# The order in which TensorE reads its operands: interleaved halves, and weights 32 bytes apart

## Chip, cores and metric

The kernel runs on one core of one Trainium2 chip. The metric is the device time of one launch in microseconds (us); lower is better. Before the change the median of three runs is 2053.01 us (2051.42 to 2057.7).

## What is computed

The reference is one layer of an encoder for one sequence of 256 tokens and 2048 features, in float32. Cut to what matters:

```python
mod = silu(c) @ ada_w + ada_b                    # shift/scale/gate, six rows of 2048
h = rms_norm(x) * (1 + scale_m) + shift_m
proj = h @ w_in                                  # q,k,v,o,i,f | qkv,z,beta,a | merge gates
y_a = (sigmoid(a_o) * norm(mlstm both ways(q, k, v, i, f))) @ w_branch_a
qkv = silu(centred depthwise conv(b_qkv))        # along the tokens, 5 taps
y_b = (norm(gated delta rule both ways(qkv, beta, a)) * silu(b_z)) @ w_branch_b
x = x + gate_m * ((g_a * y_a + g_b * y_b) @ w_out)
hf = rms_norm(x) * (1 + scale_f) + shift_f
gt, up = split(hf @ w_gate_up)
x = x + gate_f * ((silu(gt) * up) @ w_down)      # 5632 features in between
out = rms_norm(x)
```

Nearly all the arithmetic is in the products with the large weight matrices.

## The kernel before

Every large product but the first stage's is made in fp32r, a type of float32 that TensorE reads in one pass, and made precise by splitting both factors into a high and a low part: high times high, high times low, low times high, three matmuls into the same PSUM accumulator. The activations are split once (`hh`, `hl` for the block's input, `hah`/`hal`, `obh`/`obl`, `mgh`/`mgl`, `hfh`/`hfl`, `ffh`/`ffl` later); the weights are split as they arrive: a DMA on the SP queue brings 1 MB into a tile `raw` (three buffers), ScalarE copies half of it to `wh` (fp32r), VectorE subtracts to get `wl`, and TensorE reads both (three buffers each).

There are two kinds of products.

*Products by feature* (`fjob`, lines 173 to 193) give a block of 128 features by 256 tokens. The weights are the stationary operand, 128 columns, and the activation `hh[:, kk]` or `hl[:, kk]`, 256 tokens, is the moving one; 16 blocks of the contraction, three matmuls each. They serve q, k and v of the delta rule (`b_job`, 36 blocks; `gdn_conv`, line 315, copies the accumulator into a padded tile and convolves along the tokens) and q and k of the mLSTM (`a_qk`, 13 blocks; `keep_f`, line 355, copies the accumulator out and stores it).

*Products by token* (`tjob`, lines 195 to 257) give 256 tokens, two halves of 128, by 512 features. Here the activation is the stationary operand (128 tokens) and the weights, 512 columns, are the moving one. A piece of weights is `[128, 4, 512]`; `halves` (line 203) makes `wh` and `wl` for two blocks of the contraction, and 12 matmuls read them (lines 230 to 232). The last product of the output projection and of the down projection is ordered by token half (`by_token`, lines 242 to 257), one of them with 256 columns at a time. Products by token are the gates z and o, v, the two merge gates, both branch projections, the output projection, and gate, up and down of the feed-forward part.

The stages in order: a first stage to about 138 us which makes the input `hh`, `hl` and the first 16 blocks by feature in plain fp32 (line 557); the delta rule with four groups of four heads, whose small steps are interleaved by hand-written counts (`fill`, `pump`, `stream`, `drive`) with products from a list, so that TensorE always has some; the mLSTM in the same way; the branch projections; the output projection; the feed-forward part from about 1307 us; and the last norm. Rows of the modulation (`ada`) are reduced on VectorE in between.

The host side prepares the weights once, before the launch: `_blocks` for weights by feature, `_groups` (line 1449) for weights by token, and a transposition for gate and up (`gu`).

Of the kernel before, what the change touches and what calls it, by code (L numbers as in the profile page):

```python
# [9 lines left out]
F32 = mybir.dt.float32  # L10
F32R = mybir.dt.float32r
AF = mybir.ActivationFunctionType
ALU = mybir.AluOpType
PSUM = bass.MemoryType.PSUM

P = 128
T = 256
D = 2048
KB = D // P
# [33 lines left out]
def hybrid_block(ctx: ExitStack, tc: tile.TileContext, xr, nfr, crow, pk_d, cst_d, ada2, ada4, win0, winb, wint, wba, wbb, wo, wgu, wd, out, dbg=None):  # L53
    nc = tc.nc
    V, S, G, PE = nc.vector, nc.scalar, nc.gpsimd, nc.tensor

    def pool(stack, name, bufs=1, **kw):
        return stack.enter_context(tc.tile_pool(name=name, bufs=bufs, **kw))

    cp = pool(ctx, "cp")  # L60
    st = pool(ctx, "st")
# [6 lines left out]
    def big(p, dt, name):  # L68
        return p.tile([P, KB, T], dt, tag="b16", name=name)

    def order(ins, yes=True):

        return tc.keep_in_program_order(ins) if yes else ins
# [33 lines left out]
    def add():  # L107

        part, b, raw = asked.pop(0)
        c = part * KB + b  # L110
        order(V.scalar_tensor_tensor(raw, raw, 1.0, row_c[:, :D], ALU.mult, ALU.mult, accum_out=mod[:, c : c + 1]), room[0][3] > 1)  # L111
        if b == KB - 1:
            c = slice(part * KB, part * KB + KB)
            V.tensor_tensor(mod[:, c], mod[:, c], pk[:, PK_ADAB + c.start : PK_ADAB + c.stop], ALU.add)
# [21 lines left out]
    def raw_tile(shape, name):  # L136

        since[0] += 1
        if since[0] > 2 and asked and room[0][0] is st:
            add()  # L140
        return st.tile(shape, F32, tag="raw", bufs=3, name=name)
# [31 lines left out]
    def fjob(name, src, done):  # L173

        ps = acc_ps.tile([P, 512], F32, tag="acc", name=f"acc_{name}")
        o = ps[:, :T]
        raw = raw_tile([P, KB, P], f"raw_{name}")
        nc.sync.dma_start(raw, src)
        for k0 in range(0, KB, 8):
            wh = st.tile([P, 8, P], F32R, tag="wh", bufs=3, name=f"wh_{name}_{k0}")  # L180
            wl = st.tile([P, 8, P], F32R, tag="wl", bufs=3, name=f"wl_{name}_{k0}")
            S.activation(wh, raw[:, k0 : k0 + 8], AF.Copy)
            settle()
            V.tensor_tensor(wl, raw[:, k0 : k0 + 8], wh.bitcast(F32), ALU.subtract)
            for k in range(8):
                kk = k0 + k
                PE.matmul(o, wh[:, k], hh[:, kk], start=kk == 0, stop=False)  # L187
                PE.matmul(o, wh[:, k], hl[:, kk], start=False, stop=False)  # L188
                PE.matmul(o, wl[:, k], hh[:, kk], start=False, stop=kk == KB - 1)  # L189
            if k0:  # L190
                pump()
                done(o)
            yield True

    def tjob(name, chunks, xh, xl, done, early=0, by_token=None, steps=1, parts=((0, slice(0, 512)), (1, slice(0, 512)))):

        raws = {}

        def halves(u, k0):
            if u not in raws:
                raws[u] = raw_tile([P, 4, 512], f"raw_{name}_{u}")
                nc.sync.dma_start(raws[u], chunks[u])
            wh = st.tile([P, 2, 512], F32R, tag="wh", bufs=3, name=f"wh_{name}_{u}_{k0}")
            wl = st.tile([P, 2, 512], F32R, tag="wl", bufs=3, name=f"wl_{name}_{u}_{k0}")
            order(S.activation(wh, raws[u][:, k0 : k0 + 2], AF.Copy), early)  # L209
            settle()  # L210
            order(V.tensor_tensor(wl, raws[u][:, k0 : k0 + 2], wh.bitcast(F32), ALU.subtract), early)  # L211
            return wh, wl

        todo = [(u, k0) for u in range(len(chunks)) for k0 in (0, 2)]
        made = []
        for i, q in enumerate(todo[:early]):
            made.append(halves(*q))
            if steps > 1 or i == early - 1:
                yield True
        ps = [acc_ps.tile([P, 512], F32, tag="acc", name=f"acc_{name}_{t}") for t in range(2)]  # L220
        last = 4 * len(chunks) - 1
        if by_token:
            todo = todo[:-2]
        for n, (u, k0) in enumerate(todo):
            wh, wl = made.pop(0) if made else halves(u, k0)
            for k in range(2):
                kk = 4 * u + k0 + k
                for t in range(2):
                    c = slice(t * P, (t + 1) * P)
                    order(PE.matmul(ps[t], xh[:, kk, c], wh[:, k], start=kk == 0, stop=False), early and steps > 1)  # L230
                    PE.matmul(ps[t], xl[:, kk, c], wh[:, k], start=False, stop=False)  # L231
                    PE.matmul(ps[t], xh[:, kk, c], wl[:, k], start=False, stop=kk == last)  # L232
            if k0:
                pump()
                if u == len(chunks) - 1:
                    done(ps)
            yield True
            if early and steps > 1:
                if n + early < len(todo):
                    made.append(halves(*todo[n + early]))  # L240
                yield True
        if by_token:
            w = [halves(len(chunks) - 1, k0) for k0 in (0, 2)]
            by_token()
            for i, (t, part) in enumerate(parts):
                if i > 1:
                    ps.append(acc_ps.tile([P, 512], F32, tag="acc", name=f"acc_{name}_{i}"))
                c = slice(t * P, (t + 1) * P)
                o = ps[i][:, : part.stop - part.start]
                for k in range(4):  # L250
                    kk = last - 3 + k
                    wh, wl = (a[:, k % 2, part] for a in w[k // 2])
                    PE.matmul(o, xh[:, kk, c], wh, start=i == 2 and not k, stop=False)
                    PE.matmul(o, xl[:, kk, c], wh, start=False, stop=False)
                    PE.matmul(o, xh[:, kk, c], wl, start=False, stop=kk == last)
                done(t, ps[i], part)
                yield True
# [34 lines left out]
    hh = big(bigA, F32R, "hh")  # L292
    hl = big(bigA, F32R, "hl")
# [9 lines left out]
    for i in range(NP_):  # L303
        pd = fr.tile([P, T + 4], F32, name=f"pad{i}")
# [10 lines left out]
    def gdn_conv(h, j, ps):  # L315

        if j == 0:
            kq = fr.tile([P, 2, T], F32, tag="kq", bufs=2, name=f"kq{h}")
            vf = fr.tile([P, T], F32, tag="vf", bufs=2, name=f"vf{h}")
            parts[h] = (kq, vf)  # L320
            if h == 1:
                decay_load(h)
        kq, vf = parts[h]
        cb = (16 + h, h, 32 + h)[j]
        w = [pk[:, PK_CONV + 5 * cb + i : PK_CONV + 5 * cb + i + 1] for i in range(5)]
        pd = pads[npad[0] % NP_]
        npad[0] += 1
        if ps is not None:
            S.activation(pd[:, 2 : T + 2], ps, AF.Copy)
        settle(1)  # L330
        cv = fr.tile([P, T], F32, tag="cv", bufs=2, name=f"cv{h}_{j}")
        S.activation(cv, pd[:, 2 : T + 2], AF.Copy, scale=w[2])
        for i in (0, 1, 3, 4):
            V.scalar_tensor_tensor(cv, pd[:, i : i + T], w[i], cv, ALU.mult, ALU.add)

        def end():
            order(S.activation(kq[:, j] if j < 2 else vf, cv, AF.Silu))
            if ps is None:
                evict(3 * h + j + 1 + NP_)

        behind.append(end)
# [13 lines left out]
    def keep_f(dst, name):  # L355
        def done(ps):
            ev = evp.tile([P, T], F32, tag="evf", bufs=2, name=f"ev_{name}")
            S.activation(ev, ps, AF.Copy)
            S.dma_start(dst, ev)
        return done  # L360

# [127 lines left out]
    with ExitStack() as s0:  # L489
# [35 lines left out]
        ra, raw = loads(0)  # L525
# [18 lines left out]
        for b in range(KB):  # L544
            if b:
                ra, raw = loads(b)
# [445 lines left out]
    last = (0, 1, 2, 1, 2, 2, 1, 1, 3, 0)  # L992
# [386 lines left out]
    for j in range(FB // 4):  # L1379
# [4 lines left out]
        for e2 in range(2):  # L1384
            px = gps(f"pxf{j}_{e2}")
            for e in range(2):
                f = 2 * e2 + e
# [38 lines left out]
    for g in range(4):  # L1426
        c = slice(g * 512, (g + 1) * 512)
# [18 lines left out]
    return np.ascontiguousarray(w.reshape(kb, P, nb, P).transpose(2, 1, 0, 3))  # L1446


def _groups(w):
    k, n = w.shape  # L1450
    return np.ascontiguousarray(w.reshape(k // 512, 4, P, n // 512, 512).transpose(3, 0, 2, 1, 4))


def _fm(v):
# [3 lines left out]
def _arrays(x, c, ada_w, ada_b, norm_mix_w, w_in, mlstm_b_i, mlstm_b_f, mlstm_norm_w, gdn_conv_w,  # L1458
# [26 lines left out]
    w = w_in[0]  # L1485
# [5 lines left out]
    for h in range(NH_A):  # L1491
# [7 lines left out]
    win = np.concatenate([_blocks(gate, 1), _blocks(w[:, perm], 64)], 0)  # L1499
# [7 lines left out]
    gu = w_gate_up[0].reshape(4, 4, P, 2, KD, 512).transpose(4, 3, 0, 2, 1, 5)  # L1507
# [6 lines left out]
        "ada2": np.ascontiguousarray(np.concatenate([adaT[1::-1], bias], 3).transpose(1, 2, 0, 3)),  # L1514
        "ada4": np.ascontiguousarray(adaT[2:]),
        "win0": np.ascontiguousarray(win[[*range(13), 49, 50, 51]].transpose(2, 1, 0, 3)),
        "winb": np.ascontiguousarray(win[13:]),
        "wint": wint,
        "wba": _groups(w_branch_a[0]),
        "wbb": _groups(w_branch_b[0]),  # L1520
        "wo": _groups(w_out[0]),
        "wgu": np.ascontiguousarray(gu),
        "wd": _groups(w_down[0]),
    }

# [16 lines left out]
```

## Time and profile before

| | |
|---|---|
| span of the profiled execution | 2054.3 us |
| median of three runs | 2053.01 us (2051.42 to 2057.7) |
| TensorE matmuls busy | 2017.2 us |
| TensorE weight loads busy | 1698.6 us |
| VectorE busy | 1397.7 us |
| ScalarE busy | 1027.4 us |
| GpSimd busy | 116.6 us |
| read from HBM, written | 467.07 MB, 16.82 MB |
| mean granted TensorE clock | 0.992 |

The profiled execution's own time is known by its span alone, from its first to its last instruction; no separate device time of it is given. It lies inside the spread of the runs.

In the rows of the profile `PE` is a matmul, `PEld` the load of its stationary operand, and a name such as `acc_gt<-wh_gt,hfh` is the output tile and what it is made from. The end of a matmul's record is modelled, and records overlap: the distance between the starts of two matmuls is what TensorE takes for one. A shape `128x512` on a matmul is that of the moving operand.

### The profile page before, as it was taken

The page shows a single profiled execution, that of the slowest core. Times are in us where ns is not written, and L with a number is a line of the kernel's source. Part 1 is how long each engine was busy: PE and PEld are TensorE (multiplying, and loading weights), DVE is VectorE, ACT ScalarE, POOL GpSimd, SP SyncE. Part 2 cuts the span into 40 slices and gives each one's busy share as a digit, 9 for nine tenths or more (in the row PEclk, how much of TensorE's full clock was granted, in tenths as well). Part 3 has the DMA queues.
Part 4 walks back from the last instruction along what each step waited for, and adds up shares of the span by engine and source line. Part 5 has one row for each costly group of instructions (what it writes and reads, how often), then busy time and mean ns, then how long its engine had stood idle before and what let it go on. Part 6 is the DMA issues. An engine that isn't in the chain of part 4 may idle for free.

```text
span 2054.3 us, 27025 instructions
## 1 busy us (share of the span) xinstructions
PE 2017.2 (98%) x10386; PEld 1698.6 (83%) x10386; DVE 1397.7 (68%) x2062; ACT 1027.4 (50%) x1541; POOL 116.6 (6%) x211
## 2 busy tenths in 40 slices
PE   8999999999999999999999999999999999999998
PEld 6878789988997888889787888788888888878886
DVE  5778877877888788866577778756556554555554
ACT  3146647765675667455534444644444444444443
POOL 0001210111011010100100000200000000000000
PEclk9999999999999999999999999999999999999999
DMA  9986666656666666686776877466666665555553
GB/s 400 420 332 209 195 224 227 220 165 212 226 199 221 245 205 226 205 288 260 260 269 254 309 292 289 163 236 237 237 226 234 254 226 187 193 194 196 193 192 136
DMA packets 78962, 485.64 MB, mean 236 GB/s; under 512 B 10585, under 2 KB 15969, under 8 KB 24433
## 3 DMA queue, kind: packets, MB, share of 16 engines
q1 hardware_dynamic: 63216, 450.69, 60.5%
q0 software_dynamic: 8160, 17.88, 3.9%
q10 hardware_dynamic: 7458, 15.36, 2.0%
q8 instruction: 81, 1.33, 0.3%
q14 instruction: 47, 0.39, 0.1%
HBM read 467.07 MB, written 16.82 MB: 236 GB/s over the span
## 4 chain that ended last, share of the span: by engine, by line
PE 86%; DMA 6%; DVE 5%; ACT 1%; issue 1%; POOL 0%; ACTq 0%; SPq 0%; DVEq 0%; POOLq 0%
PE acc_gt L230 4%; PE acc_gt L232 4%; PE acc_gt L231 4%; PE acc_up L232 4%; PE acc_up L231 4%; PE acc_up L230 4%; PE acc_d L230 4%; PE acc_d L232 4%; PE acc_d L231 4%; DMA ra<-ada 3%; PE acc_o L232 3%; PE acc_o L230 3%; PE acc_o L231 3%; PE acc_b L187 2%; PE acc_b L188 2%; PE acc_b L189 2%
## 5 line engine op out<-in xcount | busy, mean ns | idle before, releaser
L211 DVE TENSOR_TENSOR wl_d<-raw_d,wh_d 128x1024 fp32r<-128x1024 f32 x88 | 107.9, 1226 | 119.9 <-ACT wh_d L209 119.9
L211 DVE TENSOR_TENSOR wl_up<-raw_up,wh_up 128x1024 fp32r<-128x1024 f32 x88 | 107.8, 1226 | 111.9 <-ACT wh_up L209 111.9
L211 DVE TENSOR_TENSOR wl_gt<-raw_gt,wh_gt 128x1024 fp32r<-128x1024 f32 x88 | 108.6, 1234 | 89.1 <-ACT wh_gt L209 89.1
L187 PE MATMUL acc_b<-hh,wh_b 128*128 128x256 f32 x576 | 164.7, 286 | 0.0
L209 ACT ACTIVATE wh_d<-raw_d 128x1024 fp32r<-128x1024 f32 x88 | 93.3, 1061 | 139.0 <-PE acc_d L231 134.0
L189 PE MATMUL acc_b<-hh,wl_b 128*128 128x256 f32 x576 | 160.8, 279 | 0.0
L188 PE MATMUL acc_b<-hl,wh_b 128*128 128x256 f32 x576 | 159.6, 277 | 0.0
L209 ACT ACTIVATE wh_gt<-raw_gt 128x1024 fp32r<-128x1024 f32 x88 | 93.3, 1060 | 128.7 <-PE acc_gt L231 77.3
L111 DVE SCALAR_TENSOR_TENSOR ada<-ada,crow 128x2048 f32<-128x2048 f32 x64 | 146.2, 2284 | 10.8 <-DMA ada<-ada 10.8
L209 ACT ACTIVATE wh_up<-raw_up 128x1024 fp32r<-128x1024 f32 x88 | 93.2, 1060 | 118.0 <-PE acc_up L231 84.2
L230 PE MATMUL acc_gt<-wh_gt,hfh 128*128 128x512 f32 x352 | 139.2, 395 | 0.1
L231 PE MATMUL acc_gt<-wh_gt,hfl 128*128 128x512 f32 x352 | 138.3, 393 | 0.0
L232 PE MATMUL acc_gt<-wl_gt,hfh 128*128 128x512 f32 x352 | 137.5, 391 | 0.0
L230 PE MATMUL acc_up<-wh_up,hfh 128*128 128x512 f32 x352 | 136.9, 389 | 0.0
L231 PE MATMUL acc_up<-wh_up,hfl 128*128 128x512 f32 x352 | 136.9, 389 | 0.0
L232 PE MATMUL acc_up<-wl_up,hfh 128*128 128x512 f32 x352 | 136.9, 389 | 0.0
L230 PE MATMUL acc_d<-wh_d,ffh 128*128 128x512 f32 x344 | 134.3, 391 | 0.0
L231 PE MATMUL acc_d<-wh_d,ffl 128*128 128x512 f32 x344 | 134.3, 390 | 0.0
L232 PE MATMUL acc_d<-wl_d,ffh 128*128 128x512 f32 x344 | 133.9, 389 | 0.0
L557 PE MATMUL first<-x,raw 128*128 128x256 f32 x512 | 115.9, 386 | 6.4 <-ACT x L551 6.4
L557 PEld LDWEIGHTS first<-x,raw 128*128 128x128 f32 x512 | 97.3, 192 | 25.1 <-ACT x L551 12.0
L187 PEld LDWEIGHTS acc_b<-hh,wh_b 128*128 128x128 f32 x576 | 108.4, 188 | 1.2 <-issue 0.9
(374 smaller groups left out, 5262.6 us busy)
## 6 DMA issues: line engine op xcount, KB each, us to landing
ada<-ada SPq DMA_DIRECT2D x64, 1024.0 KB, 4.9
raw_gt<-wgu SPq DMA_DIRECT2D x44, 1024.0 KB, 4.9
raw_up<-wgu SPq DMA_DIRECT2D x44, 1024.0 KB, 4.9
raw_d<-wd SPq DMA_DIRECT2D x44, 1024.0 KB, 4.8
raw_b<-winb SPq DMA_DIRECT2D x36, 1024.0 KB, 5.0
ra<-ada SPq DMA_DIRECT2D x32, 1025.0 KB, 15.3
raw<-win SPq DMA_DIRECT2D x16, 1024.0 KB, 14.5
raw_z<-wint SPq DMA_DIRECT2D x16, 1024.0 KB, 5.5
```

The costliest lines, as they stand in the source:

```text
L111: order(V.scalar_tensor_tensor(raw, raw, 1.0, row_c[:, :D], ALU.mult, ALU.mult, accum_out=mod[:, c : c + 1]), room[0][3] > 1)
L187: PE.matmul(o, wh[:, k], hh[:, kk], start=kk == 0, stop=False)
L188: PE.matmul(o, wh[:, k], hl[:, kk], start=False, stop=False)
L189: PE.matmul(o, wl[:, k], hh[:, kk], start=False, stop=kk == KB - 1)
L209: order(S.activation(wh, raws[u][:, k0 : k0 + 2], AF.Copy), early)
L211: order(V.tensor_tensor(wl, raws[u][:, k0 : k0 + 2], wh.bitcast(F32), ALU.subtract), early)
L230: order(PE.matmul(ps[t], xh[:, kk, c], wh[:, k], start=kk == 0, stop=False), early and steps > 1)
L231: PE.matmul(ps[t], xl[:, kk, c], wh[:, k], start=False, stop=False)
L232: PE.matmul(ps[t], xh[:, kk, c], wl[:, k], start=False, stop=kk == last)
L557: PE.matmul(first[o], raw[:, o], x[:, b], start=b == 0 and o % 2 == 0, stop=b == KB - 1 and o % 2 == 1)
```

## The change

Three things are read in another order; no arithmetic is changed.

1. `woven(a)` turns the columns of a moving operand into an access pattern that takes one column of the first half, then one of the second, and so on. Both kinds of products use it. For products by token the weights are reordered before the launch (`_woven`) so that the result comes out in the natural order; for products by feature the activation cannot be, so the accumulator's columns come out as pairs, and the two evictions (`gdn_conv`, `keep_f`) write them back in order.
2. In products by token the two halves lie 1024 bytes apart in a partition (256 columns of four bytes), in products by feature 512 bytes.
3. The stationary weights of products by feature lie as `[128 columns, 8 blocks]` instead of `[8 blocks, 128 columns]`. The columns of one matmul's weights are then 32 bytes apart in a partition, where they were side by side.

```diff
@@ fjob
-        raw = raw_tile([P, KB, P], f"raw_{name}")
+        raw = raw_tile([P, 2, P, 8], f"raw_{name}")
...
-            wh = st.tile([P, 8, P], F32R, tag="wh", bufs=3, name=f"wh_{name}_{k0}")
-            wl = st.tile([P, 8, P], F32R, tag="wl", bufs=3, name=f"wl_{name}_{k0}")
-            S.activation(wh, raw[:, k0 : k0 + 8], AF.Copy)
+            wh = st.tile([P, P, 8], F32R, tag="wh", bufs=3, name=f"wh_{name}_{k0}")
+            wl = st.tile([P, P, 8], F32R, tag="wl", bufs=3, name=f"wl_{name}_{k0}")
+            S.activation(wh, raw[:, k0 // 8], AF.Copy)
             settle()
-            V.tensor_tensor(wl, raw[:, k0 : k0 + 8], wh.bitcast(F32), ALU.subtract)
+            V.tensor_tensor(wl, raw[:, k0 // 8], wh.bitcast(F32), ALU.subtract)
...
-                PE.matmul(o, wh[:, k], hh[:, kk], start=kk == 0, stop=False)
-                PE.matmul(o, wh[:, k], hl[:, kk], start=False, stop=False)
-                PE.matmul(o, wl[:, k], hh[:, kk], start=False, stop=kk == KB - 1)
+                PE.matmul(o, wh[:, :, k], woven(hh[:, kk]), start=kk == 0, stop=False)
+                PE.matmul(o, wh[:, :, k], woven(hl[:, kk]), start=False, stop=False)
+                PE.matmul(o, wl[:, :, k], woven(hh[:, kk]), start=False, stop=kk == KB - 1)
             if k0:
                 pump()
-                done(o)
+                done(o.rearrange("p (c h) -> p h c", h=2))
...
+    def woven(a, n=2):
+
+        return a.rearrange("p (h c) -> p c h", h=n)
@@ tjob
-                    order(PE.matmul(ps[t], xh[:, kk, c], wh[:, k], start=kk == 0, stop=False), early and steps > 1)
-                    PE.matmul(ps[t], xl[:, kk, c], wh[:, k], start=False, stop=False)
-                    PE.matmul(ps[t], xh[:, kk, c], wl[:, k], start=False, stop=kk == last)
+                    order(PE.matmul(ps[t], xh[:, kk, c], woven(wh[:, k]), start=kk == 0, stop=False), early and steps > 1)
+                    PE.matmul(ps[t], xl[:, kk, c], woven(wh[:, k]), start=False, stop=False)
+                    PE.matmul(ps[t], xh[:, kk, c], woven(wl[:, k]), start=False, stop=kk == last)
...
-                    wh, wl = (a[:, k % 2, part] for a in w[k // 2])
+                    wh, wl = (woven(a[:, k % 2])[:, part.start // 2 : part.stop // 2] for a in w[k // 2])
@@ gdn_conv
-            S.activation(pd[:, 2 : T + 2], ps, AF.Copy)
+            S.activation(pd[:, 2 : T + 2].rearrange("p (h c) -> p h c", h=2), ps, AF.Copy)
@@ keep_f
-            S.activation(ev, ps, AF.Copy)
+            S.activation(ev.rearrange("p (h c) -> p h c", h=2), ps, AF.Copy)
@@ before the launch
+def _woven(w, n=2):
+
+    return np.ascontiguousarray(w.reshape(*w.shape[:-1], -1, n).swapaxes(-1, -2)).reshape(w.shape)
...
-    return np.ascontiguousarray(w.reshape(k // 512, 4, P, n // 512, 512).transpose(3, 0, 2, 1, 4))
+    return _woven(w.reshape(k // 512, 4, P, n // 512, 512).transpose(3, 0, 2, 1, 4))
...
-        "winb": np.ascontiguousarray(win[13:]),
+        "winb": np.ascontiguousarray(win[13:].reshape(-1, P, 2, 8, P).swapaxes(3, 4)),
...
-        "wgu": np.ascontiguousarray(gu),
+        "wgu": _woven(gu),
```

## The prediction

> **What bounds the kernel now.** I read the page's head first, then the shares of the chain that ended last, then the groups of TensorE.
>
> ```profile
> span 2054.3 us, 27025 instructions
> PE 2017.2 (98%) x10386; PEld 1698.6 (83%) x10386; DVE 1397.7 (68%) x2062; ACT 1027.4 (50%) x1541; POOL 116.6 (6%) x211
> PEclk9999999999999999999999999999999999999999
> PE 86%; DMA 6%; DVE 5%; ACT 1%; issue 1%; POOL 0%; ACTq 0%; SPq 0%; DVEq 0%; POOLq 0%
> ```
>
> TensorE is busy for 98% of the span, at its full clock in nearly every slice, and 86% of the chain runs through it. So the kernel lasts as long as its products follow one another. The span, 2054.3 us, is 1.3 us above the median of the runs (2053.0) and inside their spread; I sum against the span and carry differences over to the median.
>
> The groups of the products, by the first of their three lines (lines 231, 232 and 188, 189 have the same counts):
>
> ```profile
> L230 PE MATMUL acc_gt<-wh_gt,hfh 128*128 128x512 f32 x352 | 139.2, 395 | 0.1
> L230 PE MATMUL acc_up<-wh_up,hfh 128*128 128x512 f32 x352 | 136.9, 389 | 0.0
> L230 PE MATMUL acc_d<-wh_d,ffh 128*128 128x512 f32 x344 | 134.3, 391 | 0.0
> L230 PE MATMUL acc_yb<-wh_yb,obh 128*128 128x512 f32 x128 | 51.9, 406 | 0.0
> L230 PE MATMUL acc_ya<-wh_ya,hah 128*128 128x512 f32 x128 | 51.6, 403 | 0.0
> L230 PE MATMUL acc_o<-wh_o,mgh 128*128 128x512 f32 x120 | 46.8, 390 | 0.0
> L230 PE MATMUL acc_ma<-wh_ma,hh 128*128 128x512 f32 x128 | 51.9, 405 | 0.0
> L230 PE MATMUL acc_z<-wh_z,hh 128*128 128x512 f32 x128 | 51.2, 400 | 2.5 <-ACT wh_z L209 2.5
> L230 PE MATMUL acc_v<-wh_v,hh 128*128 128x512 f32 x128 | 51.0, 399 | 0.0
> L230 PE MATMUL acc_o<-wh_o,hh 128*128 128x512 f32 x128 | 50.9, 397 | 0.0
> L230 PE MATMUL acc_mb<-wh_mb,hh 128*128 128x512 f32 x128 | 50.6, 396 | 0.0
> L187 PE MATMUL acc_b<-hh,wh_b 128*128 128x256 f32 x576 | 164.7, 286 | 0.0
> L187 PE MATMUL acc_a<-hh,wh_a 128*128 128x256 f32 x208 | 59.8, 288 | 0.0
> ```
>
> Per line there are 352+352+344+128+128+120 = 1424 products by token on later activations and 5 x 128 = 640 on the block's input hh, hl: 4272 and 1920 with the three lines. By feature there are 576+208 = 784, so 2352. The 389 ns of one record is no price: records overlap. The price is the step from one start to the next, which the timeline of TensorE gives. Columns: start, duration, engine, line.
>
> ```profile
> 299.81 0.39 PE L232 MATMUL acc_o<-wl_o,hh 128*128 128x512 f32 x1
> ...
> 302.79 0.39 PE L230 MATMUL acc_o<-wh_o,hh 128*128 128x512 f32 x1
> ...
> 1499.62 0.39 PE L232 MATMUL acc_gt<-wl_gt,hfh 128*128 128x512 f32 x1
> ...
> 1503.93 0.39 PE L230 MATMUL acc_gt<-wh_gt,hfh 128*128 128x512 f32 x1
> ```
>
> Between the first two lie 13 steps, 2.98 us: 229.2 ns. Between the last two 19 steps, 4.31 us: 226.8 ns. The same for 256 columns, two stretches of products by feature and one of products by token, the split last ones of the output projection:
>
> ```profile
> 399.91 0.28 PE L187 MATMUL acc_b<-hh,wh_b 128*128 128x256 f32 x1
> ...
> 401.50 0.28 PE L189 MATMUL acc_b<-hh,wl_b 128*128 128x256 f32 x1
> ...
> 600.68 0.28 PE L187 MATMUL acc_b<-hh,wh_b 128*128 128x256 f32 x1
> ...
> 602.91 0.28 PE L188 MATMUL acc_b<-hl,wh_b 128*128 128x256 f32 x1
> ...
> 1300.36 0.28 PE L253 MATMUL acc_o<-wh_o,mgh 128*128 128x256 f32 x1
> ...
> 1302.64 0.28 PE L254 MATMUL acc_o<-wh_o,mgl 128*128 128x256 f32 x1
> ```
>
> Steps: 1.59/14 = 113.6 ns, 2.23/19 = 117.4 ns and 2.28/19 = 120.0 ns. By feature I take the middle, 115.5. Together the changed products hold 4272 x 0.2268 + 1920 x 0.2292 + 2352 x 0.1155 = 969 + 440 + 272 = 1681 us of the span. Every nanosecond per step of 512 columns is worth 6.2 us.
>
> **How fast could a step be?** Two rows of the chain in order of time bound it:
>
> ```profile
> 357.12 1.72 PE ks L630 x4
> 985.88 2.57 PE pden L950 x24
> ```
>
> Line 630 is a product in plain fp32, 512 columns, half the pace: 1.72/4 = 430 ns a record. Half of it, 215 ns, is my estimate for 512 columns in fp32r when nothing disturbs (107.5 for 256). Line 950 moves one column per record, so 2.57/24 = 107.1 ns is the loading of 128 columns of weights. Today's steps are above the estimate by 11.8 ns (late) and 14.2 ns (early) for 512 columns, by 12.5 ns for 256 columns by token, by 6.1 to 9.9 ns by feature. The excess by token is the same for 256 columns as for 512: it is a price per product, not per column. What happens once per product is the load of the next 128 weights, beside the moving read. I read the excess as the two reads of SBUF getting into each other's way; the half-pace product leaves room between its reads.
>
> **The change, part by part.** It adds and removes no product, no DMA, no wait, and reorders nothing; the weights come in the same pieces, reordered before the launch. Four things move.
>
> (1) The moving read of products by token takes its 512 columns alternately from two places 1024 bytes apart. No row of the trace shows TensorE reading so. The ends: the whole excess goes, 4272 x 11.8 + 1920 x 14.2 = 50 + 27 = 78 us gained; or it runs at the half pace of line 630, 430 ns: 4272 x 203.2 + 1920 x 200.8 = 868 + 386 = 1254 us lost. I take the gaining end. For it speaks that the excess is per product: the moving stream by itself already keeps its pace, and two streams, each called on half as often, leave every fetch twice the time before its next bytes are due, which is the room that a colliding weight load needs.
>
> (2) The moving read of products by feature alternates between places 512 bytes apart. A step cannot fall much: the weight load alone takes 107.1 ns of 113.6 to 117.4. Ends: 2352 x 8.0 = 19 us gained, or the half pace, 2352 x 99.5 = 234 us lost. I take a third of the gain, 6 us, since the load fills the whole step.
>
> (3) The stationary weights by feature are read 32 bytes apart. Their record now:
>
> ```profile
> L187 PEld LDWEIGHTS acc_b<-hh,wh_b 128*128 128x128 f32 x576 | 108.4, 188 | 1.2 <-issue 0.9 <-ACT wh_mb L209 0.2
> ```
>
> Ends: no change of the 107.1 ns, or twice it, 214 ns per step: 2352 x 98.7 = 232 us. I take none, since the load moves one column per 0.84 ns (107.1/128), half the rate of the moving read, and has more time for each.
>
> (4) 49 evictions read PSUM with every second column and write halves:
>
> ```profile
> L329 ACT ACTIVATE pad<-acc_b 128x256 f32<-128x256 f32 x36 | 13.5, 374 | 2.9 <-PE acc_b L189 2.7
> L358 ACT ACTIVATE ev_a<-acc_a 128x256 f32<-128x256 f32 x13 | 4.8, 373 | 5.9 <-PE acc_a L189 5.8
> ```
>
> Ends: unchanged, or doubled, 13.5 + 4.8 = 18 us of ScalarE, which is 50% busy, with four accumulators in turn. I cost it at nothing; without that cover 18 us.
>
> Would faster products starve? The feeders per 12 products:
>
> ```profile
> L209 ACT ACTIVATE wh_d<-raw_d 128x1024 fp32r<-128x1024 f32 x88 | 93.3, 1061 | 139.0 <-PE acc_d L231 134.0
> L211 DVE TENSOR_TENSOR wl_d<-raw_d,wh_d 128x1024 fp32r<-128x1024 f32 x88 | 107.9, 1226 | 119.9 <-ACT wh_d L209 119.9
> ```
>
> Twelve products take 2.72 us now and 2.58 us at 215 ns; ScalarE needs 1.06 us of it and VectorE 1.23 us, and ScalarE waits for TensorE to release its buffer. They follow. In the stages of the delta rule other chains end some of the waits, so I count 86% (TensorE's share of the chain): 0.86 x (78 + 6) = 72 us. 2053.0 - 72 = 1981 us.
>
> [...] The nearest row of any strided read in this trace is VectorE's, in the triangular inversion (line 698): thirty elements each 128 bytes from the next, and thirty side by side.
>
> ```profile
> 264.74 0.20 DVE L698 TENSOR_TENSOR uu<-uu,utmp 64x30 f32<-64x30 f32 x1
> ...
> 298.00 0.18 DVE L698 TENSOR_TENSOR uu<-uu,utmp 64x30 f32<-64x30 f32 x1
> ```
>
> Apart costs 0.02 us more, 0.7 ns an element with rounding as large as half of that; it reads and writes so, and the row cannot tell which of them pays. If such a price held for TensorE's reads, (1) to (3) would end near their bad ends. [...]
>
> **Rivals.** [...]
>
> *B, only the weight load pays for its 32 bytes.* Then products by feature become bound by the load, at up to 214 ns: 232 us more. With the gain by token, 0.86 x 78 = 67 us, that is 2218 us; without it 2285 us. [...] Against: the load has 0.84 ns per column. It decides once the load takes over about 136 ns: then 2352 x 28.5 = 67 us are eaten.
>
> *C, the excess is tied to the weight load alone* and does not care for the order of the moving columns: steps stay, 2053 us. For it: it is per product.
>
> *D, alternating makes collisions twice as many*: a second excess by token, 78 us more, 2131 us.
>
> **Numbers.** Forecast, faster, 0.50; A 0.20; B 0.17; C 0.08; D 0.05. About 0.3%, 6 us, is what a measurement can tell here. Faster 0.50, same 0.08, slower 0.42. The forecast's own range is 1950 (all 78 + 19 us and a little idle time) to 2045; with B (to 2290), C and D 1950 to 2290 holds 0.80; A is left out.
>
> **What would show it.** Right: in the feed-forward stage the step by token falls from 226.8 to 215 to 219 ns, by feature to 108 to 115, weight load records stay at 188 ns, evictions near 374 ns. [...] B: steps by feature and their weight loads grow, by token they fall. C: same steps. Wrong altogether if steps by token and by feature move in a way that the span does not follow.

## The result: slower by 10.6%

The changed kernel takes 2270.27 us (median, 2267.62 to 2273.3), the kernel before, run beside it, 2053.79 us. The ratio is 1.1057, 95% interval 1.1039 to 1.1074. The forecast was 1981 us with a gain; what came is rival B, which the prediction put at 2218 us with a chance of 0.17: products by token became faster, products by feature became bound by the load of their weights.

The head of the page of after and the shares of its chain answer to the first lines shown of before:

```profile
span 2267.9 us, 27027 instructions
PE 2232.8 (98%) x10386; PEld 1995.7 (88%) x10386; DVE 1397.6 (62%) x2062; ACT 1025.1 (45%) x1541; POOL 116.6 (5%) x211
PEclk9999999999999999999999999999999999999999
PE 89%; DMA 4%; DVE 4%; ACT 1%; issue 1%; POOL 0%; ACTq 0%; SPq 0%; DVEq 0%; POOLq 0%
```

TensorE is busy for 98% of the span as before, with the same 10386 products at the same granted clock (0.993, before 0.992), and VectorE and ScalarE do the same work (1397.6 and 1025.1 us, before 1397.7 and 1027.4). Only TensorE grew: products by 215.6 us, weight loads by 297.1 us, the span by 213.6 us. So the loss is in the products themselves and not in a wait. The groups of after (partitions x elements, count | busy us, mean ns) say which:

```profile
L234 PE MATMUL acc_gt<-wh_gt,hfh 128*128 128x512 f32 x352 | 135.4, 385 | 0.2 <-ACT hfh L1338 0.2
L187 PE MATMUL acc_b<-hh,wh_b 128*128 128x256 f32 x576 | 236.9, 411 | 0.0
L187 PEld LDWEIGHTS acc_b<-hh,wh_b 128*128 128x128 f32 x576 | 192.9, 335 | 0.9 <-issue 0.5 <-ACT pad L333 0.2
L333 ACT ACTIVATE pad<-acc_b 128x256 f32<-128x256 f32 x36 | 13.5, 375 | 43.8 <-PE acc_b L189 43.7
L362 ACT ACTIVATE ev_a<-acc_a 128x256 f32<-128x256 f32 x13 | 4.8, 373 | 20.2 <-PE acc_a L189 20.2
```

By token a record is 385 ns, before 395. By feature it is 411 ns, before 286, and the record of the weight load 335 ns, before 188. The evictions stay at 375 and 373 ns (374 and 373); ScalarE only waits longer ahead of them, 43.8 us for 2.9. The same wait is seen one stage up, where ScalarE converts the weights by feature and must have a buffer back from TensorE. The waits of ScalarE (us in total, times, longest), first of before, then of after:

```profile
ACT wh_b L182 <- PE acc_b L188: 25.3, 20, 2.8
```

```profile
ACT wh_b L182 <- PE acc_b L188: 140.7, 39, 5.6
```

The feeder is idle behind TensorE more than five times as long: nothing upstream is late. The price of a product is the step between starts. Two stretches of TensorE's timeline by token, then one by feature (start, duration in us):

```profile
559.63 0.38 PE L234 MATMUL acc_o<-wh_o,hh 128*128 128x512 f32 x1
...
564.59 0.38 PE L236 MATMUL acc_o<-wl_o,hh 128*128 128x512 f32 x1
...
1744.63 0.38 PE L236 MATMUL acc_gt<-wl_gt,hfh 128*128 128x512 f32 x1
...
1748.73 0.38 PE L234 MATMUL acc_gt<-wh_gt,hfh 128*128 128x512 f32 x1
```

```profile
329.70 0.40 PE L188 MATMUL acc_b<-hl,wh_b 128*128 128x256 f32 x1
...
335.94 0.40 PE L187 MATMUL acc_b<-hh,wh_b 128*128 128x256 f32 x1
```

By token 4.96/23 = 215.7 ns early and 4.10/19 = 215.8 ns late, for 229.2 and 226.8 ns before. By feature 6.24/26 = 240.0 ns, for 113.6 to 117.4 ns before. For the whole kernel I added up the time from each start on TensorE to the next, by the kind of the product (pauses ahead of the next product included). By token are lines 230 to 232 of before, 234 to 236 of after; the 60 split last products are among all other:

| us, start to start | by token | by feature | all other | last start |
|---|---|---|---|---|
| before | 1436.3 | 287.2 | 318.2 | 2044.2 |
| after | 1370.4 | 569.5 | 315.1 | 2257.7 |
| difference | -65.9 | +282.3 | -3.1 | +213.5 |

The differences make +213.3 us, and the span grew by 213.6 us. A gain by token and a loss by feature of four times its size are the whole result.

### The profile page after: what moved, and what is told of

It reads as the page before. It is cut to its first block, busy times and chain, and to the rows that moved or that the text cites. A ratio compares the mean times of both kernels' runs of the same rounds, so it can differ in the third digit from the quotient of the medians.

```text
span 2267.9 us, 27027 instructions
## 1 busy us (share of the span) xinstructions
PE 2232.8 (98%) x10386; PEld 1995.7 (88%) x10386; DVE 1397.6 (62%) x2062; ACT 1025.1 (45%) x1541; POOL 116.6 (5%) x211
## 4 chain that ended last, share of the span: by engine, by line
PE 89%; DMA 4%; DVE 4%; ACT 1%; issue 1%; POOL 0%; ACTq 0%; SPq 0%; DVEq 0%; POOLq 0%
PE acc_b L187 6%; PE acc_b L188 6%; PE acc_b L189 6%; PE acc_gt L234 3%; PE acc_gt L235 3%; PE acc_gt L236 3%; PE acc_up L235 3%; PE acc_up L236 3%; PE acc_up L234 3%; PE acc_d L236 3%; PE acc_d L235 3%; PE acc_d L234 3%; DMA ra<-ada 3%; PE acc_o L236 2%; PE acc_o L234 2%; PE acc_o L235 2%
## 5 line engine op out<-in xcount | busy, mean ns | idle before, releaser
L187 PE MATMUL acc_b<-hh,wh_b 128*128 128x256 f32 x576 | 236.9, 411 | 0.0
L189 PE MATMUL acc_b<-hh,wl_b 128*128 128x256 f32 x576 | 233.3, 405 | 0.0
L188 PE MATMUL acc_b<-hl,wh_b 128*128 128x256 f32 x576 | 232.6, 404 | 0.0
L189 PEld LDWEIGHTS acc_b<-hh,wl_b 128*128 128x128 f32 x576 | 193.9, 337 | 0.5 <-DVE cv L338 0.2
L188 PEld LDWEIGHTS acc_b<-hl,wh_b 128*128 128x128 f32 x576 | 193.9, 337 | 0.3
L187 PEld LDWEIGHTS acc_b<-hh,wh_b 128*128 128x128 f32 x576 | 192.9, 335 | 0.9 <-issue 0.5
L215 DVE TENSOR_TENSOR wl_d<-raw_d,wh_d 128x1024 fp32r<-128x1024 f32 x88 | 107.7, 1224 | 109.2 <-ACT wh_d L213 109.2
L182 ACT ACTIVATE wh_b<-raw_b 128x1024 fp32r<-128x1024 f32 x72 | 75.9, 1055 | 167.5 <-PE acc_b L188 140.7
L184 DVE TENSOR_TENSOR wl_b<-raw_b,wh_b 128x1024 fp32r<-128x1024 f32 x72 | 87.6, 1217 | 94.0 <-ACT wh_b L182 94.0
```

Source lines behind the costliest of these rows:

```text
L182: S.activation(wh, raw[:, k0 // 8], AF.Copy)
L184: V.tensor_tensor(wl, raw[:, k0 // 8], wh.bitcast(F32), ALU.subtract)
L187: PE.matmul(o, wh[:, :, k], woven(hh[:, kk]), start=kk == 0, stop=False)
L188: PE.matmul(o, wh[:, :, k], woven(hl[:, kk]), start=False, stop=False)
L189: PE.matmul(o, wl[:, :, k], woven(hh[:, kk]), start=False, stop=kk == KB - 1)
```

## Experiments

The expectations number the theories. The first is that the parts simply add: the alternating read by token brings the gain, and the weights 32 bytes apart alone bring the loss. Its rivals put the loss, or some of it, on the alternating moving read by feature, or on two parts meeting. Four kernels with one part each, or all but one, tell them apart. The kernel before, beside these four, had a median of 2052.75 us.

**Products by token alone.** Only line 230 and its fellows read alternately, with the order of those weights changed before the launch; products by feature, their weights and the evictions are as before.

```
-  order(PE.matmul(ps[t], xh[:, kk, c], wh[:, k], ...
+  order(PE.matmul(ps[t], xh[:, kk, c], woven(wh[:, k]), ...
   (and the two lines below it, the split last chunk, wba, wbb, wo, wgu, wd)
```

> Only the products by token read their moving weights alternately; products by feature are as before. Separate prices (theory 1: alternating takes away the excess that the weight load costs the moving read; the loss of the changed kernel is the weight load 32 bytes apart): step by token 216 ns instead of 227 to 229, 6228 steps x 11.7 ns = 73 us less, 1980 us. Theory 2 (the loss comes from the alternating moving read of the products by feature): the same 1980 us. Theory 3 (the loss needs both strided reads at once): the same.

Measured: 1993.58 us (1991.66 to 1995.93), ratio 0.9717, interval 0.9703 to 0.9732. Its page, and the weight load by feature from its groups:

```profile
span 1990.3 us, 27025 instructions
```

```profile
L187 PEld LDWEIGHTS acc_b<-hh,wh_b 128*128 128x128 f32 x576 | 108.4, 188 | 1.3 <-issue 0.5 <-ACT wh_b L182 0.4 <-ACT kq L341 0.2
```

The load is 188 ns as before. Start to start, products by token take 1371.2 us (-65.1), by feature 288.0 and all other 318.3: the gain of after is here whole, and nothing else moves. The median fell by 59.2 us; 73 us, and so 1980 us, had been expected, and what is missing isn't traced further.

**Weights by feature apart, alone.** All moving reads and the evictions are as before.

```
-  wh = st.tile([P, 8, P], ...);   PE.matmul(o, wh[:, k], hh[:, kk], ...
+  wh = st.tile([P, 1, P, 8], ...); PE.matmul(o, wh[:, k // 8, :, k % 8], hh[:, kk], ...
```

> Only the stationary weights by feature lie 32 bytes apart; all moving reads are side by side. Theory 1: step by feature about 240 ns as in the changed kernel, 2352 x 124 ns = 292 us more, 2345 us, weight load record 337 ns. Theory 2: steps by feature 113 to 118 ns, 2053 us. Theory 3: the load alone takes twice its 107 ns, 214 ns per step, 2285 us.

Measured: 2334.58 us, ratio 1.1377 (1.1361 to 1.1394). Its span and its load by feature:

```profile
span 2332.5 us, 27025 instructions
```

```profile
L187 PEld LDWEIGHTS acc_b<-hh,wh_b 128*128 128x128 f32 x576 | 193.7, 336 | 0.9 <-issue 0.5 <-ACT pad L329 0.2
```

The loss of after is here whole, with a moving read side by side: 572.8 us by feature (+285.6), the load's record 336 ns. By token the sum is 1431.5 us, 4.8 us less than before with the same steps: some pauses are gone, which I did not trace further. The time is 10 us under the 2345 us that the first theory gave.

**The alternating read by feature alone**, with the evictions that put the columns back in order.

```
-  PE.matmul(o, wh[:, k], hh[:, kk], ...
+  PE.matmul(o, wh[:, k], woven(hh[:, kk]), ...
-  done(o)
+  done(o.rearrange("p (c h) -> p h c", h=2))
   (and lines 329 and 358 as in the change)
```

> Only the products by feature read their moving activations alternately and their evictions put the columns back; weights side by side, products by token as before. Theory 1: step by feature falls to the load's floor, 111 to 112 ns, 2352 x 4 ns = 9 us less, 2044 us. Theory 2: steps of 240 ns, 2345 us. Theory 3: as theory 1. If the evictions with every second column cost ScalarE more than 374 ns, it shows here alone.

Measured: 2049.66 us, ratio 0.999 (0.9979 to 1.0001): no difference that can be told from none (2044 us had been expected).

```profile
L187 PEld LDWEIGHTS acc_b<-hh,wh_b 128*128 128x128 f32 x576 | 110.6, 192 | 1.2 <-issue 1.0 <-ACT wh_mb L213 0.2
L333 ACT ACTIVATE pad<-acc_b 128x256 f32<-128x256 f32 x36 | 13.5, 374 | 2.5 <-PE acc_b L189 2.3
```

Steps by feature fall to 112 ns and no further, and sum to 285.9 us (-1.3). The evictions cost nothing.

**Both alternating reads, weights as before**: the change without its third part.

```
-  wh = st.tile([P, P, 8], ...);  PE.matmul(o, wh[:, :, k], woven(hh[:, kk]), ...
+  wh = st.tile([P, 8, P], ...);  PE.matmul(o, wh[:, k], woven(hh[:, kk]), ...
```

> Both kinds of products read alternately, weights by feature side by side: the change without its third part. Theory 1: 216 ns by token, 112 ns by feature, 73 + 9 = 82 us less, 1971 us. Theory 2: 1980 + 292 = 2272 us. Theory 3: 1971 us.

Measured: 1996.02 us, ratio 0.9731 (0.9707 to 0.9755), 25 us above what was expected. The steps are the expected ones, 216 and 112 ns, but the pauses between products grew, so the sums fell by less.

```profile
span 1993.3 us, 27027 instructions
```

By token 1375.3 us, by feature 284.2, other 320.7. It can't be told from products by token alone, so the by-feature reads bring nothing. From these four the first theory stands in its causes and its rivals fall: -64.0 us of span (by token alone) and +278.2 us (weights alone) add up to +214.2 us, and after has +213.6 us. So close a sum is partly luck, since the profiled execution of before is one of its longer ones: 2054.3 us, against 2047.8 to 2053.6 us of the 13 executions beside these four. By the medians, each against the kernel before beside it, the parts are -59.2 and +281.8 us, together +222.7 us, and after has +216.5 us. Products by token alone is the simplest of the fast versions, faster than both kernels of this case.

**How far apart is too far?** Weights 32 bytes apart bring the whole loss; two kernels with weights 8 and 16 bytes apart show how it goes with the distance. Both have both alternating reads, with 2 or 4 blocks of weights interleaved and not 8. Theory B in their expectations has weights pay more the farther apart they lie; the expectation of the first small kernel, further down, has it in full. The kernel before beside them: 2053.66 us.

```
   q = 2 (8 bytes) or 4 (16 bytes)
   raw = raw_tile([P, KB // q, P, q]);  wh = st.tile([P, 8 // q, P, q])
   PE.matmul(o, wh[:, k // q, :, k % q], woven(hh[:, kk]), ...
```

> As both kinds woven, but the weights by feature 8 bytes apart (two blocks interleaved). [...] Theory B or any price per byte of distance: steps above 112 ns, about 130 to 180 ns, 2040 to 2160 us.

> As both kinds woven, but the weights by feature 16 bytes apart (four blocks interleaved). [...] Theory B or a price per byte of distance: between, 150 to 210 ns, 2080 to 2220 us.

Measured, 8 bytes: 2000.38 us, ratio 0.9735 (0.9708 to 0.9762). 16 bytes: 2261.65 us, ratio 1.1011 (1.0995 to 1.1028). The load by feature, 8 bytes and then 16:

```profile
L187 PEld LDWEIGHTS acc_b<-hh,wh_b 128*128 128x128 f32 x576 | 113.4, 197 | 1.3 <-issue 0.7 <-ACT wh_b L182 0.3 <-ACT wh_mb L213 0.2
```

```profile
L187 PEld LDWEIGHTS acc_b<-hh,wh_b 128*128 128x128 f32 x576 | 189.8, 330 | 1.0 <-issue 0.5 <-ACT pad L333 0.2
```

And a stretch of TensorE's timeline with 16 bytes:

```profile
329.69 0.40 PE L188 MATMUL acc_b<-hl,wh_b 128*128 128x256 f32 x1
...
335.81 0.40 PE L187 MATMUL acc_b<-hh,wh_b 128*128 128x256 f32 x1
```

At 16 bytes the step is 6.12/26 = 235.4 ns, close to the 240 ns at 32. At 8 bytes it is 118 to 120 ns, against 112 side by side: 5 to 7% more. So it isn't reading apart as such that costs most, nor mainly how far: nearly the whole loss comes between 8 and 16 bytes, and no distance between was tried. Theory B falls at both: 8 bytes cost less than its 2040 to 2160 us, and 16 bytes more than its 2080 to 2220 us.

**A step by itself.** Two small kernels leave the layer out and run TensorE alone, 48 products of each sort in a row, on weights and moving columns that stay in SBUF. Their code, shortened:

```
def st(s, i, cols):     # weights: s columns from one to the next
    wt[:, :P * s].rearrange("p (c s) -> p c s", s=s)[:, :cols, i % s]
def moving(h, i, n):    # h parts read in turns, column by column
    mv[:, i % 4, :n].rearrange("p (h c) -> p c h", h=h)
near:  "p (b h c) -> p b c h", h=2     # parts only 8 to 128 bytes apart
for i in range(48): PE.matmul(ps, st(s, i, cols), moving(h, i, n), ...)
```

> Not the layer: runs of 48 fp32r products each, back to back, over the same tiles, one operand's order changed per run; its output is a copy of a weight and means nothing, its time neither; the steps are read. [...] Theory B (banks: places far enough apart are read in turn without loss): weights pay more the farther apart, and moving reads cost the same however many parts alternate, 216 ns, only parts very near each other lose. On the excess of the plain product: if it is the collision with the weight load, 64 weight columns halve it (220 ns at 512 moving columns) and 32 quarter it (217 ns); if it is a price of the moving read alone, it stays at 227 ns.

The chain in order of time (start, us for 48 products). Side by side; 2, 4, 8, 16 parts in turn; 128 and 256 parts (columns 16 and 8 bytes apart); two parts 8 and 16 bytes apart; 64 and 32 columns of weights:

```profile
27.79 10.88 PE acc_plain L55 x48
38.67 10.36 PE acc_mvtwo L55 x48
49.03 13.59 PE acc_mvfour L55 x48
62.62 23.39 PE acc_mveight L55 x48
86.00 20.88 PE acc_mvsixteen L55 x48
...
148.38 22.15 PE acc_mvline L55 x48
170.53 21.66 PE acc_mvpairs L55 x48
192.19 10.90 PE acc_neara L55 x48
203.09 10.36 PE acc_nearb L55 x48
...
244.53 11.04 PE acc_whalf L55 x48
255.57 11.12 PE acc_wquarter L55 x48
```

10.88/48 = 226.7 ns and 10.36/48 = 215.8 ns: the two steps of the kernel, with nothing else running. So its excess came neither from the engines around nor from DMA. Two parts bring it down at 16, 32, 64, 128 and 1024 bytes; at 8 bytes they don't (227.1 ns). With 4 parts the step is 283 ns, with 8 it is 487, with 16 it is 435, and 32 and 64 parts stay there (433 and 431 ns): the bad end of part (1), 430 ns, is reached from 8 parts on, and theory B, 216 ns for any number of parts, falls here too. Moving columns 16 bytes apart take 461 ns and 8 bytes apart 451 ns: the 8 bytes that cost the weights 5 to 7% double the step of a moving read. A smaller weight load doesn't help: 230.0 and 231.7 ns with 64 and 32 columns.

Weights apart, 256 moving columns: side by side; alternating; then 8, 16, 32, 64 and 128 bytes apart; 32 bytes again with a moving read side by side; 32 bytes with 512 alternating columns:

```profile
266.69 5.76 PE acc_short L55 x48
272.45 5.36 PE acc_shortwoven L55 x48
277.81 5.76 PE acc_sttwo L55 x48
283.56 11.20 PE acc_stfour L55 x48
294.76 11.52 PE acc_steight L55 x48
306.28 10.65 PE acc_stsixteen L55 x48
316.93 10.58 PE acc_stthirtytwo L55 x48
327.51 11.57 PE acc_steightplain L55 x48
339.08 11.73 PE acc_steightlong L55 x48
```

120.0, 111.7, 120.0, 233.3, 240.0, 221.9, 220.4, 241.0 and 244.4 ns. The loss by feature is reproduced alone, 240 ns at 32 bytes, with either moving read. The last row shows that such a load doesn't hide behind 512 moving columns either: 244.4 ns for 215.8.

The second small kernel has 32 columns of weights (a load's record was 109 ns with them in the first, 188 ns with 128), and varies the number of moving columns. It also alternates by 2, 4 and 8 columns at a time (128 columns of weights).

> Not the layer: runs of 48 fp32r products, as in the first run of steps; its output is a copy of a weight and its time means nothing. With 32 weight columns, so that the load cannot bound, 64 to 512 moving columns side by side and in two alternating halves. [...] Theory P (the prediction's: a price per product): side by side 120 ns at 256, 173 at 384, 227 at 512; by four and by eight 216 ns as any alternation. [...]

128, 256 and 512 columns, side by side and alternating; then turns of 2, 4 and 8 columns; last 512 columns with weights 8 bytes apart, side by side and alternating:

```profile
31.17 2.88 PE acc_plquarter L59 x48
34.05 2.68 PE acc_woquarter L59 x48
36.73 5.66 PE acc_plhalf L59 x48
42.39 5.24 PE acc_wohalf L59 x48
...
63.74 11.12 PE acc_plfull L59 x48
74.87 10.36 PE acc_wofull L59 x48
...
95.59 15.76 PE acc_bytwo L59 x48
111.35 12.00 PE acc_byfour L59 x48
123.35 11.68 PE acc_byeight L59 x48
...
157.23 11.21 PE acc_stsixplain L59 x48
168.43 10.36 PE acc_stsixwoven L59 x48
```

Side by side 60.0, 117.9 and 231.7 ns, alternating 55.8, 109.2 and 215.8 ns. The excess is 4.2, 8.7 and 15.9 ns (10.8 at 384 columns): it grows with the columns. The slopes, (231.7 - 60.0)/384 = 0.447 and (215.8 - 55.8)/384 = 0.417 ns per column, say the same. Turns of 2, 4 and 8 columns take 328, 250 and 243 ns, all more than the plain product of the same run (227.3 ns). Theory P, one price per product, falls by the growing excess, and by turns of 4 and 8, for which it gave 216 ns. With weights 8 bytes apart the product side by side takes 233.5 ns (227.3 with weights side by side) and the alternating one 215.8 ns: the weights can still add some 6 ns to a plain read.

## Why the prediction was wrong, point by point

**What bounds the kernel**: right. TensorE is the bound before and after, and its starts account for 213.3 of 213.6 us.

**Part (3), the weights 32 bytes apart: the step that failed.** "I take none, since the load moves one column per 0.84 ns, half the rate of the moving read, and has more time for each." At 32 bytes a column costs 240.0/128 = 1.88 ns, so a load of 128 columns becomes the whole step. That is above even the far end of 214 ns: twice the load's 107.1 ns was no bound, only a guess at one. The term was 0 and is +282 us. The argument compared two rates, both of operands read side by side; it had no row of TensorE reading weights apart. The nearest one it had, VectorE's, had the sign (0.20 us for 0.18). The prediction itself says that such a price would bring part (3) near its bad end, and still put the term at nothing. Its 0.7 ns an element on top of 0.84 ns per column would have given 1.5 ns a column.

**Part (1), the alternating read by token: right in size, wrong in reason.** 78 us at most, 67 after the factor of 86%; the starts give -65.9 us in after, and products by token alone shortened the span by 64.0 us and the median by 59.2 us. The floor of 215 ns, half the 430 ns of one record in plain fp32, is 215.8. (Such a product leaves two records, 512 for the 256 products of line 557, one in fp32r a single one, 576 for the 36 x 16 of `acc_b` on line 187.) But the excess is not, in the main, a collision with the weight load: cutting the load to a quarter doesn't cut it (231.7 ns for 226.7), and it grows with the number of columns (4.2 ns at 128, 15.9 ns at 512). That the number came out is luck in part. The sign that I leaned on, the same excess at 256 columns (12.5 ns) as at 512, was false: with the same weights an alternating product of 256 columns takes 111.7 ns and not 107.5, so the real excess there is 8 ns; the split products fell to 112 ns in after. Why two halves in turn are faster stays open: that every fetch then has twice the time was my reading, and no run shows it.

**Part (2), the moving read by feature**: a gain of 6 us was taken, 1.3 us of steps is seen, and the time of that kernel can't be told from before. The reason given, that the load fills the step, holds in part: with a quarter of the weights the alternating step is 109.2 ns for 111.7, so the moving read itself needs nearly as long.

**Part (4), the evictions**: right, 375 and 373 ns.

**The rivals.** B holds at the 32 bytes it names, and at 16; at 8 bytes the weights hardly pay. It missed 2270 by 52 us, 50 of them by feature: 282 us where its 214 ns a step gave 232. Its condition was mis-added: 28.5 ns more than today's step of 115.5 ns is 144 ns, not 136. A (0.20), which expected the half pace of every alternating read, falls for two parts (215.8 ns); half the pace and worse shows from 8 parts on. C falls (steps moved) and D falls (they moved down). The range, 1950 to 2290, holds 2270 only because B was in it.

**What is left open.** Moving columns cost 451/512 = 0.88 ns each at 8 bytes apart and 461/512 = 0.90 ns at 16, while weights hardly pay at 8 and take twice the step at 16; the runs don't say why. Nor do they say why turns of 2 columns cost 328 ns and turns of one 216, why 8 parts cost more than 16, why fewer weight columns make a plain product slower, or why the pauses between products grew in the two fast versions.

## What to carry to other kernels

Lay out stationary weights so that neighbouring columns lie side by side: 8 bytes apart cost little (118 to 120 ns for 112), 16 and 32 bytes apart double the step of a product of 256 columns (235 and 240 ns), and at 32 bytes one of 512 columns went from 216 to 244 ns. Moving fp32r columns in turns, one by one, from exactly two halves brought 5% a step here and 2.8% of this kernel; measure such a pattern alone before going to four parts or to turns of two. A bound such as "twice what it takes now" is none until a row shows it.

## What the runs showed of the hardware that I had not expected

- A moving fp32r read side by side isn't the fastest: 226.7 ns for 512 columns, 215.8 ns when two halves take turns.
- The pattern is narrow: 4, 8 and 16 parts take 283, 487 and 435 ns, turns of 2 columns 328 ns, columns 8 bytes apart 451 ns.
- With weights 16 and 32 bytes apart a product of 256 columns takes 233 to 240 ns, and a little less, 222 and 220 ns, at 64 and 128; at 8 bytes 118 to 120 ns.
- A smaller weight load makes a product slightly longer, not shorter: 226.7 ns with 128 columns of weights, 230.0 with 64, 231.7 with 32.
- ScalarE reads PSUM in steps of two columns at no cost: 374 and 375 ns.
